# Fused 512-column passes for memory queries, memory keys, u and four query/key pairs, and a plan with longer margins

## The chip, the cores and the metric

The kernel runs on one core of a Trainium2 chip. Its time is the device time of one execution in microseconds (us). Before the change it was 557.04 us, the median of three runs (556.15 to 557.11). One further execution was taken by the hardware profiler; the profile and the trace come from it.

The core's engines run side by side, each with its own queue of instructions, and wait for one another through semaphores. PE (TensorE) does matmuls and writes their results into PSUM, a small memory of 8 banks of 128 partitions x 512 fp32 numbers. DVE (VectorE) and ACT (ScalarE) do the elementwise work and read PSUM and SBUF, POOL (GpSimd) does little here, and SP (SyncE) issues most of the transfers from the chip's main memory.

## The reference

Two layers over x of 256 positions x 1024, each a token mixer beside a cross-attention into 256 memory tokens, an output projection, a LayerNorm, and a SwiGLU feed-forward part with another LayerNorm. Everything is fp32.

```python
for i in range(DEPTH):                       # 2 layers
    if i == 0:
        u, v, q_mem = split(x @ a_w_in, [768, 1536])
        mix = gmlp_mixer(u, v, ...)          # gelu(u) * (W_s layer_norm(gelu(v)) + b), chunks of 128
    else:
        q, k, v, q_mem = split(x @ b_w_in, [768, 1536, 2304])
        mix = moba_attention(q, k, v)        # 12 heads of 64; one block of 256: causal attention
    mem_out = memory_cross_attention(q_mem, mem, w_mem_kv[i])      # 4 heads of 64
    sub = concatenate([mix, mem_out]) @ w_mix_out[i]
    x = layer_norm(ALPHA * x + sub, ...)
    x = layer_norm(ALPHA * x + swiglu(x, w_ffn_in[i], w_ffn_out[i]), ...)   # D_FF 2816
```

## The kernel before

**Precision.** TensorE works on a shorter format (fp32r). So `split(hi, lo, src)` makes two parts of every fp32 operand: ScalarE casts src into hi, VectorE subtracts hi from src into lo. A product is three matmuls into one PSUM tile, `PASSES = ((0, 0), (0, 1), (1, 0))`: hi by hi, hi by lo, lo by hi. In the profile ScalarE's casts and VectorE's subtractions into tiles named `spl_...` are the splits of weights, the costliest groups of both engines.

**Projections.** The projections that come out transposed (features on the partitions, the 256 positions along a row) go through `ws_proj`: for every block of 128 weight columns and each of KT = 8 slices of the model dimension, three matmuls, each with 128x128 weights as the stationary operand and 256 columns of tokens as the moving one:

```python
for j in cols:
    for k in range(KT):
        for n, (a, b) in enumerate(PASSES):
            mm(pst[:, j % pst.shape[1], :], stream.rows(w, k, KT)[:, a, j * P:(j + 1) * P], xs(b, k), ...)
```

The token tile xT (x2T in layer 1) holds hi and lo of a slice next to each other, 512 columns in all; memT, the memory tokens, held them as (hi or lo, slice, position) before. `ws_proj` makes the memory queries (tiles hqm; from them qqm, scaled and split by `stack_q`), the memory keys (hkm; kkm and klm by `stack_k`), u of layer 0 (pu; then gelu into uT) and the queries and keys of layer 1 (qk). Each pair hp of heads in layer 1 takes two blocks of 128 columns, `qk_half(hp, 0)` the queries and `qk_half(hp, 1)` the keys; `stack_q` and `stack_k` make hi (ScalarE, into qks) and lo (VectorE, into qks and klq) of them out of PSUM, and `scores` multiplies them (tiles s).

**Stages, with their place in the profiled span.** v of layer 0 until 22.45 us, then hqm, u, hkm, the gMLP gate (sv), values of the memory (pvm) and scores (sm); from 61.88 the output projection of layer 0 (opa), one `step` for each slice of 128 mixed features and one half (tt) of the positions, with its last slices in `close`, and between the steps the memory attention's transposes (ptm) and its products with the values (pvm); LayerNorm; from about 100 the feed-forward part of layer 0. There `product` forms seven Strassen-like products for each pair of column chunks (M1 to M7, tiles Xf, Yf, Zf), `m1f` and `m5f` are the gated results (m5f by a VectorE instruction that wants sgf from ScalarE), `tpf` their transposes on TensorE, htf the split transposes, and fof the output sums. Layer 1 begins at about 262 (bv, then hqm at 291.74, qk and attention until 345) and ends with its own output projection (opc) and feed-forward part (names in g).

**The order.** Nothing runs as the code is written, except on TensorE. `Plan` records every instruction, and `Plan.order` then simulates the kernel with a cost for each instruction and a model of the transfers (`Wire`). TensorE's order is the program's. For the other engines `simulate` takes, whenever an engine is free, the ready instruction with the earliest due time, or lets a more urgent one that is soon ready go first, depending on three numbers (slip, idle, margin). It does so for every entry of `TRIALS` and keeps the order in which TensorE loses least by the model. `Wire.SPARE` is the margin, in ns, by which a transfer from SyncE or from GpSimd is taken to land later than modelled. Copies and scalings (`nc.copy`, `nc.scale`) may go to ScalarE or to VectorE, and the plan chooses. All planned instructions are issued on one line, L590, so the profile's rows must be told apart by their tiles.

Of the kernel before, what the change touches and what calls it, by code (L numbers as in the profile page):

```python
# [13 lines left out]
F32 = mybir.dt.float32  # L14
F32R = mybir.dt.float32r
BF16 = mybir.dt.bfloat16
AF = mybir.ActivationFunctionType
# [4 lines left out]
P = 128  # L22
D = 1024
T = 256
# [222 lines left out]
class Wire:  # L247

    HARD, SOFT, BOTH, LANES = ((7000, 250), (30000, 370), (1e12, 428)), 223, (155, 123), 8
    SPARE, SKEW = (600, 800), 2000  # L250

    def __init__(self):
        self.now, self.hard, self.soft, self.sent = 0.0, [], [], []
# [36 lines left out]
class Plan:  # L290


    ENGINES = ("tensor", "vector", "scalar", "gpsimd", "sync")
    TRIALS = ((150, 1500, 800), (150, 1000, 500), (300, 1500, 1200), (100, 700, 300), (300, 2500, 1600))

    def __init__(self, nc, pools, space):
        self.nc, self.pools, self.space, self.ops, self.trials = nc, pools, space, [], []
# [102 lines left out]
    def simulate(self, slip, idle, margin):  # L400
# [73 lines left out]
        while len(out) < len(self.ops):  # L474
            best, again = None, False
            for e in self.ENGINES:
                if e == "tensor":
                    if ip == len(pe) or waiting[pe[ip].n]:
                        continue
                    cands = [pe[ip]]  # L480
                else:
                    cands = ready[e]
                c = [(max(free[e], t), op) for op in cands for t in (opening(op, e),) if t is not None]
                if not c:
                    continue
                t0 = min(t for t, _ in c)
                first = [x for x in c if x[0] <= t0 + 1]
                t, op = min(first, key=lambda x: (x[1].late, x[1].n))

                me = op.calls()[e]  # L490
                if e in by_late:
                    u = by_late[e]
                    while head[e] < len(u) and u[head[e]] in gone:
                        head[e] += 1
                    soon, memo = None, {}
                    for o2 in u[head[e]:head[e] + 40]:
                        if o2.late >= op.late:
                            break
                        if o2 in gone or not waiting[o2.n] or t + me.hold <= o2.late + lost - margin:
                            continue  # L500
                        r = hope(o2, memo, 4)
                        if t < r < t + me.hold and (soon is None or r < soon[0]):
                            soon = r, o2
                    for t2, o2 in c:
                        if t < t2 < t + me.hold and o2.late < op.late and t + me.hold > o2.late + lost - margin and (
                                soon is None or t2 < soon[0]):
                            soon = t2, o2
                    if soon:
                        r, o2 = soon
                        short = [x for x in c if x[0] + x[1].calls()[e].hold <= r + slip and x[1] is not op]  # L510
                        if short:
                            t, op = min(short, key=lambda x: (x[1].late, x[1].n))
                        elif r + o2.hold + me.hold < op.late + lost and r - busy[e] < idle:
# [170 lines left out]
def build(chip, tc, ins, out):  # L684
    ET = mybir.EngineType
    with (
# [18 lines left out]
        def mm_tile(name):  # L705
            return tile_of("ps", [P, 512], F32, "mm", name, 4)
# [78 lines left out]
        def ws_proj(pst, w, xs, cols=(0, 1)):  # L785
# [4 lines that stand above are left out]
                        mm(pst[:, j % pst.shape[1], :], stream.rows(w, k, KT)[:, a, j * P:(j + 1) * P], xs(b, k),  # L790
                           k == 0 and n == 0, k == KT - 1 and n == 2)

        def ts_pass(pst, xs, wsl, tt, first, last):

            for n, (a, b) in enumerate(PASSES):
                mm(pst, xs(a)[:, tt * P:(tt + 1) * P], wsl(b), first and n == 0, last and n == 2)
# [155 lines left out]
            stream.done(name)  # L952
            return t

        def mem_q(name, xs):
            qa = [tile_of("act", [P, 2, T], F32R, f"qm{c}", f"q{name}{c}") for c in range(2)]
            t = proj_t(name, xs)
            for c in range(2):
                stack_q(lambda par: qa[c][:, par, :], t[:, c, :])
            return qa  # L960

        def mem_k(name, memx):
            ka = [tile_of("act", [P, 2, T], F32R, f"mix{6 + c}", f"k{name}{c}") for c in range(2)]
            t = proj_t(name, memx)
            for c in range(2):
                stack_k(lambda par: ka[c][:, par, :], klm[:, c], t[:, c, :])
            return ka, klm

        def acc_mms(acc, lhs, rhs, first, last):
# [263 lines left out]
        memT = []  # L1233

        def memx(s, k):
            return memT[k // 2][:, s, k % 2, :]

        stream.get("qm0", 1)
        gv = raw_tile("gv").rearrange("p (a c) -> p a c", a=2)[:, :, :W_MIX]
# [23 lines left out]
        qm = mem_q("qm0", xs)  # L1263
        stv = [sm(f"stv{tt}", 18)[:, :12] for tt in range(2)]
        for h in range(2):
            for tt in range(2):
# [2 lines left out]
                nc.vector.bn_stats(stv[tt][:, 6 * h:6 * h + 6], vn[:, tt, sl])  # L1269
        uT = []  # L1270
        for i in range(3):
            pu = mm_tile(f"pu{i}").rearrange("p (j t) -> p j t", j=2)
            ws_proj(pu, f"u{i}", xs)
            stream.done(f"u{i}")
            uT.append(work_tile(f"uT{i}"))
            nc.scalar.activation(uT[i], flat(pu), AF.Gelu_apprx_tanh)
        for j in range(4):
            if j % 2 == 0:
                both = tile_of("spl", [P, 2, 1024], F32R, "spl", f"memT{j}", HALF_BUFS)
            t = both[:, j % 2, :].rearrange("p (s n) -> p s n", s=2)  # L1280
            split(t[:, 0, :], t[:, 1, :], mraws[j])
            memT.append(t.rearrange("p s (k t) -> p s k t", k=2))
        km = mem_k("km0", memx)
        for tt in range(2):
            mv = sm(f"mvv{tt}", 2)
# [33 lines left out]
            nc.sync.dma_start(xres[tt], ins["x"][tt * P:(tt + 1) * P, :])  # L1319
        gb = load_gb(0, "mix")  # L1320
        op.step(0, [2, 3, 4, 5])
        pts = mem_transposes(pr, "0")
        op.step(1, [0], first=True)
        mem_pv(pts, vm, mix, "0")
        op.step(1, [1])
        op.close(0, [6, 7], xres, gb)
        x1T = tile_of("act", [P, KT, 2, T], F32R, "xT", "x1T")
        op.step(1, range(2, 6))
        op.close(1, [6, 7], xres, gb)
        A = {}  # L1330
        transpose_x(0, xres, x1T, "a", A)
# [16 lines left out]
        for tt in range(2):  # L1348
# [189 lines left out]
```

## Time and profile before

| | before |
|---|---|
| time, median of three runs | 557.04 us (556.15 to 557.11) |
| the profiled execution: its time | 556.42 us |
| its span (first to last recorded work) | 554.7 us |
| instructions on DVE / ACT | 665 / 571 |
| DMA, bytes moved | 132.51 MB, mean 239 GB/s |

The rows of the profile name an engine, an operation and tiles (output<-inputs, buffer numbers left out), then shapes and counts. A chain row gives start, length, engine, tile and number; a timeline row start, length, engine, line, operation, tiles, number, and in brackets idle time ahead of it with what ended it.

### The profile page before, as it was taken

Reading aid. Unit: us, or ns where it says so; the run is one execution under the profiler, and the core shown is the slowest. Engines: PE = TensorE matmul, PEld = TensorE weight load, DVE = VectorE, ACT = ScalarE, POOL = GpSimd, SP = SyncE. Lnnn points to the kernel's source line nnn. Section 1 sums busy time; section 2 is a strip of 40 time slices with the busy share of each in tenths; the row PEclk is TensorE's granted clock in tenths of the full one; section 3 lists DMA queues with packets and bytes.
Section 4 is the critical chain, followed back from the end, with each engine's and each line's share of the span. In section 5 each row is a group of like instructions: output and inputs, shape, how many; then the busy total and the mean of one; then the engine's idle time right before and its main releaser. Section 6 shows DMA issues by size and latency. Waiting matters only on the chain.

```text
span 554.7 us, 7993 instructions
## 1 busy us (share of the span) xinstructions
PE 545.8 (98%) x3028; PEld 473.4 (85%) x3028; DVE 502.1 (91%) x665; ACT 371.0 (67%) x571; POOL 34.3 (6%) x45
## 2 busy tenths in 40 slices
PE   9999999999999999999999999999999999999994
PEld 8999979888888888787899999888788888888884
DVE  5899969999999998989996888889999999989985
ACT  6867846785748495766555999846857585857620
POOL 2120000000000010000000000100000000001001
PEclk9999999999999999999999999999999999999998
DMA  8999843666897969889658232692678989797902
GB/s 294 403 384 381 330 171 115 191 186 222 200 421 165 380 178 324 273 251 353 231 206 325 77 114 78 211 283 77 161 259 223 419 158 417 160 371 201 284 1 77
DMA packets 23494, 132.51 MB, mean 239 GB/s; under 512 B 2592, under 2 KB 6304, under 8 KB 9376
## 3 DMA queue, kind: packets, MB, share of 16 engines
q1 hardware_dynamic: 20000, 109.45, 50.5%
q0 software_dynamic: 3024, 22.02, 21.3%
q8 instruction: 24, 0.39, 0.3%
q10 hardware_dynamic: 432, 0.52, 0.3%
q14 instruction: 14, 0.11, 0.1%
HBM read 120.46 MB, written 1.05 MB: 219 GB/s over the span
## 4 chain that ended last, share of the span: by engine, by line
PE 72%; DVE 14%; DMA 7%; issue 4%; ACT 2%; SPq 0%; DVEq 0%; ACTq 0%; POOLq 0%
PE fog L590 11%; PE Xg L590 10%; DVE spl_s_M L590 7%; PE qk L590 6%; PE Zg L590 5%; DMA raw_s<-in_w 4%; PE opc L590 4%; PE opa L590 4%; PE pu L590 3%; PE bv L590 3%; PE pvm L590 3%; PE Yg L590 2%; PE va L590 2%; PE hkm L590 2%; PE hqm L590 2%
## 5 line engine op out<-in xcount | busy, mean ns | idle before, releaser
L590 DVE TENSOR_TENSOR spl_s_M<-raw_s,spl_s_M 128x1024 fp32r<-128x1024 f32 x140 | 164.7, 1221 | 6.3 <-ACT spl_s_M L590 6.1
L590 ACT CAST spl_s_M<-raw_s 128x1024 fp32r<-128x1024 f32 x140 | 139.6, 1050 | 38.1 <-DMA raw_s<-in_w 23.4
L590 PE MATMUL fof<-spl_w,htf 128*128 128x512 f32 x264 | 63.9, 392 | 0.0
L590 PE MATMUL fog<-spl_w,htg 128*128 128x512 f32 (+1 forms) x282 | 63.9, 378 | 0.0
L590 ACT CAST spl_w<-raw_w 128x1024 fp32r<-128x1024 f32 x44 | 45.6, 1051 | 23.4 <-DMA raw_w<-in_w 20.9
L590 PEld LDWEIGHTS fog<-spl_w,htg 128*128 128x128 f32 x282 | 50.2, 188 | 9.4
L590 PEld LDWEIGHTS fof<-spl_w,htf 128*128 128x128 f32 x264 | 49.0, 188 | 9.9
L590 DVE TENSOR_TENSOR spl_w<-raw_w,spl_w 128x1024 fp32r<-128x1024 f32 x44 | 53.7, 1221 | 2.9 <-ACT spl_w L590 2.9
L590 DVE TENSOR_TENSOR raw_s<-raw_s,raw_s 128x2048 f32<-128x2048 f32 x19 | 43.5, 2288 | 0.1
L590 PE MATMUL qk<-x2T,spl_qk 128*128 128x256 f32 x288 | 36.3, 283 | 0.0
L590 PEld LDWEIGHTS qk<-x2T,spl_qk 128*128 128x128 f32 x288 | 35.2, 192 | 0.0
L590 PE MATMUL Zg<-spl_s_M,SgM 128*128 128x512 f32 x120 | 29.1, 390 | 0.0
L590 PE MATMUL Xg<-spl_s_M,SgM 128*128 128x512 f32 x120 | 29.0, 390 | 0.0
L590 PE MATMUL Zf<-spl_s_M,SfM 128*128 128x512 f32 x120 | 29.0, 390 | 0.0
L590 PE MATMUL Xf<-spl_s_M,SfM 128*128 128x512 f32 x120 | 28.8, 389 | 0.0
L590 PE MATMUL Xf<-spl_s_M,x1T 128*128 128x512 f32 x120 | 28.3, 390 | 0.0
L590 PE MATMUL Xg<-spl_s_M,x3T 128*128 128x512 f32 x120 | 28.3, 390 | 0.1
L590 PEld LDWEIGHTS Xf<-spl_s_M,x1T 128*128 128x128 f32 x120 | 22.4, 188 | 5.2 <-issue 0.6
L590 PEld LDWEIGHTS Xg<-spl_s_M,x3T 128*128 128x128 f32 x120 | 22.5, 188 | 5.1 <-issue 0.4
L590 PEld LDWEIGHTS Zg<-spl_s_M,SgM 128*128 128x128 f32 x120 | 22.5, 188 | 5.0 <-DVE SgM L590 0.4
L590 PEld LDWEIGHTS Xf<-spl_s_M,SfM 128*128 128x128 f32 x120 | 22.5, 188 | 4.7
L590 PEld LDWEIGHTS Xg<-spl_s_M,SgM 128*128 128x128 f32 x120 | 22.4, 188 | 4.8 <-DVE SgM L590 0.2
(246 smaller groups left out, 1007.8 us busy)
## 6 DMA issues: line engine op xcount, KB each, us to landing
raw_s<-in_w SPq DMA_DIRECT2D x40, 1024.0 KB, 7.7
raw_w<-in_w SPq DMA_DIRECT2D x22, 1024.0 KB, 8.6
raw_s<-in_w POOLq DMA_DIRECT2D x11, 1024.0 KB, 9.0
raw_s<-raw_s POOLq DMA_DIRECT2D x10, 1024.0 KB, 7.6
raw_o<-in_w SPq DMA_DIRECT2D x8, 1024.0 KB, 7.7
raw_qk<-in_w SPq DMA_DIRECT2D x6, 1024.0 KB, 5.4
raw_u<-in_w SPq DMA_DIRECT2D x3, 1024.0 KB, 11.6
raw_bv<-in_w SPq DMA_DIRECT2D x4, 768.0 KB, 8.1
```

Source lines behind the costliest of these rows:

```text
L590: getattr(getattr(self.nc, c.engine), c.name)(*map(real, c.args), **{k: real(v) for k, v in c.kw.items()})
```

## The change

`joint` takes the place of `ws_proj` in 22 blocks of 128 weight columns: for each slice, one matmul of weight hi by the 512 columns token hi and token lo, then one of weight lo by the 256 columns token hi, into the first half of the PSUM tile. A copy (on ScalarE or VectorE) takes the second half out and a VectorE add adds the first to it, in an SBUF tile `sum_...` (three buffers; for u the tile uT itself). `stack_q`, `stack_k` and the gelu then read SBUF. The last two pairs of heads (hp 4 and 5) stay as they were. memT is laid out anew, so that hi and lo of a slice are 512 columns in a row. `SPARE`, `TRIALS` and a rule of `simulate` change too, and in layer 0 the memory transposes and the products with the values come in two pieces.

```diff
-    SPARE, SKEW = (600, 800), 2000
+    SPARE, SKEW = (1600, 2000), 2000
...
-    TRIALS = ((150, 1500, 800), (150, 1000, 500), (300, 1500, 1200), (100, 700, 300), (300, 2500, 1600))
+    TRIALS = ((0, 700, 100), (150, 700, 100), (150, 700, 300), (0, 700, 500), (150, 700, 500))
...
-                me = op.calls()[e]
+                hold = op.calls()[e].hold
+                if e == "scalar" and op.name == "activation" and op.args[2] not in (AF.Identity, table):
+                    hold += 1283
...
+        def joint(name, w, xk, j, tile, out):
+
+            pst = tile(name)
+            for k in range(KT):
+                rw = stream.rows(w, k, KT)[:, :, j * P:(j + 1) * P]
+                mm(pst, rw[:, 0], xk(k).rearrange("p s t -> p (s t)"), k == 0, False)
+                mm(pst[:, :T], rw[:, 1], xk(k)[:, 0, :], False, k == KT - 1)
+            nc.copy(out, pst[:, T:])
+            nc.vector.tensor_add(out, out, pst[:, :T])
+
+        def sum_tile(name):
+            return tile_of("act", [P, T], F32, "sum", f"sum_{name}", 3)
...
-            t = proj_t(name, xs)
             for c in range(2):
-                stack_q(lambda par: qa[c][:, par, :], t[:, c, :])
+                t = sum_tile(f"{name}{c}")
+                joint(f"h{name}{c}", name, xk, c, mm_tile, t)
+                stack_q(lambda par: qa[c][:, par, :], t)
...
-            pu = mm_tile(f"pu{i}").rearrange("p (j t) -> p j t", j=2)
-            ws_proj(pu, f"u{i}", xs)
+            uT.append(work_tile(f"uT{i}"))
+            for j in range(2):
+                half = uT[i][:, j * T:(j + 1) * T]
+                joint(f"pu{i}{j}", f"u{i}", lambda k: xT[:, k], j, mm_tile, half)
+                nc.scalar.activation(half, half, AF.Gelu_apprx_tanh)
             stream.done(f"u{i}")
-            uT.append(work_tile(f"uT{i}"))
-            nc.scalar.activation(uT[i], flat(pu), AF.Gelu_apprx_tanh)
...
-            t = both[:, j % 2, :].rearrange("p (s n) -> p s n", s=2)
-            split(t[:, 0, :], t[:, 1, :], mraws[j])
-            memT.append(t.rearrange("p s (k t) -> p s k t", k=2))
+            t = both[:, j % 2, :].rearrange("p (k s t) -> p k s t", k=2, s=2)
+            split(t[:, :, 0, :], t[:, :, 1, :], mraws[j].rearrange("p (k t) -> p k t", k=2))
+            memT.append(t)
...
-        pts = mem_transposes(pr, "0")
+        pts = mem_transposes(pr, "0", (0, 1))
         op.step(1, [0], first=True)
-        mem_pv(pts, vm, mix, "0")
+        pts += mem_transposes(pr, "0", (2, 3))
+        mem_pv(pts, vm, mix, "0", (0,))
         op.step(1, [1])
+        mem_pv(pts, vm, mix, "0", (1,))
+        op.step(1, [2])
         op.close(0, [6, 7], xres, gb)
...
-        qm = mem_q("qm1", xs)
+        qm = mem_q("qm1", lambda k: x2T[:, k])
...
-            t = (acc_tile if j else mm_tile)(f"qk{hp}{j}")[:, :T].rearrange("p (j t) -> p j t", j=1)
-            ws_proj(t, f"qk{hp}", xs, (j,))
-            t = t[:, 0, :]
+            if hp < 4:
+                t = sum_tile(f"qk{hp}{j}")
+                joint(f"qk{hp}{j}", f"qk{hp}", lambda k: x2T[:, k], j, acc_tile if j else mm_tile, t)
+            else:
+                t = (acc_tile if j else mm_tile)(f"qk{hp}{j}")[:, :T].rearrange("p (j t) -> p j t", j=1)
+                ws_proj(t, f"qk{hp}", xs, (j,))
+                t = t[:, 0, :]
```

(`mem_k` changes like `mem_q`.)

Three places show what the change does to the order of the engines. The first is TensorE in layer 0's output projection, after step 5 of the first half of the positions. opa are the two PSUM tiles of the second half, pm the softmax of one memory head, pTm its transpose in SBUF, svm the memory's values; equal rows that follow in the same group of three passes are left out. Before:

```order
L590 MATMUL ptm_927<-ident,pm_843 128x128 x4
L590 MATMUL ptm_932<-ident,pm_867 128x128 x4
L590 MATMUL ptm_939<-ident,pm_879 128x128 x4
L590 MATMUL ptm_946<-ident,pm_895 128x128 x4
L590 MATMUL opa_953<-spl_o_0_0_595,mix_0_764 128x512
L590 MATMUL opa_957<-spl_o_0_0_595,mix_0_764 128x512
L590 MATMUL pvm_963<-pTm_935,svm_864 64x256
L590 MATMUL pvm_963<-pTm_942,svm_864 64x256
L590 MATMUL pvm_970<-pTm_949,svm_864 64x256
L590 MATMUL pvm_970<-pTm_955,svm_864 64x256
L590 MATMUL opa_953<-spl_o_0_1_605,mix_1_769 128x512
L590 MATMUL opa_957<-spl_o_0_1_605,mix_1_769 128x512
```

Of the changed kernel:

```order
L592 MATMUL ptm_861<-ident,pm_821 128x128 x4
L592 MATMUL ptm_871<-ident,pm_840 128x128 x4
L592 MATMUL opa_878<-spl_o_0_0_565,mix_0_697 128x512
L592 MATMUL opa_882<-spl_o_0_0_565,mix_0_697 128x512
L592 MATMUL ptm_894<-ident,pm_851 128x128 x4
L592 MATMUL ptm_901<-ident,pm_864 128x128 x4
L592 MATMUL pvm_906<-pTm_880,svm_784 64x256
L592 MATMUL pvm_906<-pTm_884,svm_784 64x256
L592 MATMUL opa_878<-spl_o_0_1_580,mix_1_704 128x512
L592 MATMUL opa_882<-spl_o_0_1_580,mix_1_704 128x512
L592 MATMUL pvm_928<-pTm_908,svm_784 64x256
L592 MATMUL pvm_928<-pTm_911,svm_784 64x256
```

The four heads' transposes are two and two now, with a step of the output projection between them, and the two products pvm are a step apart.

The second place is VectorE in the feed-forward part of layer 0, where chunk 7's m5f is gated (the row SCALAR_TENSOR_TENSOR). spl_w_7_0 is a weight of the output sums, raw_s and spl_s_9_M are weights of the next pair's products. Before:

```order
L590 TENSOR_TENSOR spl_w_7_0_2172<-raw_w_7_2101,spl_w_7_0_2172 128x1024
L590 TENSOR_TENSOR raw_s_9_11_2091<-raw_s_9_11_2091,raw_s_9_12_2117 128x2048
L590 TENSOR_TENSOR spl_s_9_M_0_2201<-raw_s_9_21_2138,spl_s_9_M_0_2201 128x1024
L590 SCALAR_TENSOR_TENSOR m5f_2056<-m5f_2056,sgf_2211 128x512
L590 TENSOR_TENSOR spl_s_9_M_0_2217<-raw_s_9_11_2091,spl_s_9_M_0_2217 128x1024
L590 TENSOR_TENSOR spl_s_9_M_1_2224<-raw_s_9_11_2091,spl_s_9_M_1_2224 128x1024
```

Of the changed kernel:

```order
L592 TENSOR_TENSOR spl_w_7_0_2123<-raw_w_7_2046,spl_w_7_0_2123 128x1024
L592 TENSOR_TENSOR raw_s_9_11_2038<-raw_s_9_11_2038,raw_s_9_12_2062 128x2048
L592 SCALAR_TENSOR_TENSOR m5f_2003<-m5f_2003,sgf_2151 128x512
L592 TENSOR_TENSOR spl_s_9_M_0_2156<-raw_s_9_21_2082,spl_s_9_M_0_2156 128x1024
L592 TENSOR_TENSOR spl_s_9_M_0_2164<-raw_s_9_11_2038,spl_s_9_M_0_2164 128x1024
L592 TENSOR_TENSOR spl_s_9_M_1_2171<-raw_s_9_11_2038,spl_s_9_M_1_2171 128x1024
```

m5f has moved up by one weight split.

The third is the same instruction for the last pair of that part, chunk 9, among the splits of the weights of v in layer 1 (spl_bv). Before:

```order
L590 TENSOR_TENSOR spl_w_10_1_2408<-raw_w_10_2328,spl_w_10_1_2408 128x1024
L590 TENSOR_TENSOR spl_bv_0_2417<-raw_bv_2344,spl_bv_0_2417 128x768
L590 TENSOR_TENSOR spl_bv_1_2425<-raw_bv_2344,spl_bv_1_2425 128x768
L590 TENSOR_TENSOR spl_bv_0_2457<-raw_bv_2380,spl_bv_0_2457 128x768
L590 SCALAR_TENSOR_TENSOR m5f_2311<-m5f_2311,sgf_2469 128x512
L590 TENSOR_TENSOR spl_bv_1_2474<-raw_bv_2380,spl_bv_1_2474 128x768
```

Of the changed kernel:

```order
L592 TENSOR_TENSOR spl_w_10_1_2361<-raw_w_10_2276,spl_w_10_1_2361 128x1024
L592 TENSOR_TENSOR spl_bv_0_2381<-raw_bv_2292,spl_bv_0_2381 128x768
L592 TENSOR_TENSOR spl_bv_1_2387<-raw_bv_2292,spl_bv_1_2387 128x768
L592 SCALAR_TENSOR_TENSOR m5f_2251<-m5f_2251,sgf_2407 128x512
L592 TENSOR_TENSOR spl_bv_0_2412<-raw_bv_2323,spl_bv_0_2412 128x768
L592 TENSOR_TENSOR spl_bv_1_2420<-raw_bv_2323,spl_bv_1_2420 128x768
```

Here, too, one weight split stands behind m5f now that stood ahead of it.

Elsewhere, VectorE has 22 adds and 11 copies more (of sum_qm three, sum_km two, sum_qk six), and 8 copies of 512 columns in the feed-forward parts and of svm went from VectorE to ScalarE. ScalarE also has the other 11 copies (six of uT, one sum_qm, two sum_km, two sum_qk). On SyncE's queue layer 0's raw_vm stands behind two loads of bs, and xres ahead of gb0mix.

More of the change, by code (lines that the diff above doesn't have):

```diff
@@ L498, in simulate @@
                             break
-                        if o2 in gone or not waiting[o2.n] or t + me.hold <= o2.late + lost - margin:
+                        if o2 in gone or not waiting[o2.n] or t + hold <= o2.late + lost - margin:
                             continue
                         r = hope(o2, memo, 4)
-                        if t < r < t + me.hold and (soon is None or r < soon[0]):
+                        if t < r < t + hold and (soon is None or r < soon[0]):
                             soon = r, o2
                     for t2, o2 in c:
-                        if t < t2 < t + me.hold and o2.late < op.late and t + me.hold > o2.late + lost - margin and (
+                        if t < t2 < t + hold and o2.late < op.late and t + hold > o2.late + lost - margin and (
                                 soon is None or t2 < soon[0]):
@@ L512, in simulate @@
                             t, op = min(short, key=lambda x: (x[1].late, x[1].n))
-                        elif r + o2.hold + me.hold < op.late + lost and r - busy[e] < idle:
+                        elif r + o2.hold + hold < op.late + lost and r - busy[e] < idle + hold - op.calls()[e].hold:
                             free[e] = r
@@ L953, in proj_t, with mem_q @@
             return t
-        def mem_q(name, xs):
+        def mem_q(name, xk):
             qa = [tile_of("act", [P, 2, T], F32R, f"qm{c}", f"q{name}{c}") for c in range(2)]
-            t = proj_t(name, xs)
             for c in range(2):
-                stack_q(lambda par: qa[c][:, par, :], t[:, c, :])
+                t = sum_tile(f"{name}{c}")
+                joint(f"h{name}{c}", name, xk, c, mm_tile, t)
+                stack_q(lambda par: qa[c][:, par, :], t)
+            stream.done(name)
             return qa
@@ L963, in mem_k @@
             ka = [tile_of("act", [P, 2, T], F32R, f"mix{6 + c}", f"k{name}{c}") for c in range(2)]
-            t = proj_t(name, memx)
             for c in range(2):
-                stack_k(lambda par: ka[c][:, par, :], klm[:, c], t[:, c, :])
+                t = sum_tile(f"{name}{c}")
+                joint(f"h{name}{c}", name, lambda k: memT[k // 2][:, k % 2], c, mm_tile, t)
+                stack_k(lambda par: ka[c][:, par, :], klm[:, c], t)
+            stream.done(name)
             return ka, klm
@@ L1235, in memx @@
         def memx(s, k):
-            return memT[k // 2][:, s, k % 2, :]
+            return memT[k // 2][:, k % 2, s, :]
         stream.get("qm0", 1)
@@ L1261, in build @@
                 nc.sync.dma_start(bsB[i][j * HD:(j + 1) * HD], ins["bs"][j:j + 1, 2 * i:2 * i + 2, :].to_broadcast([HD, 2, P]))
-        qm = mem_q("qm0", xs)
+        qm = mem_q("qm0", lambda k: xT[:, k])
         stv = [sm(f"stv{tt}", 18)[:, :12] for tt in range(2)]
@@ L1321, in build @@
         op.step(0, [2, 3, 4, 5])
-        pts = mem_transposes(pr, "0")
+        pts = mem_transposes(pr, "0", (0, 1))
         op.step(1, [0], first=True)
-        mem_pv(pts, vm, mix, "0")
+        pts += mem_transposes(pr, "0", (2, 3))
+        mem_pv(pts, vm, mix, "0", (0,))
         op.step(1, [1])
+        mem_pv(pts, vm, mix, "0", (1,))
+        op.step(1, [2])
         op.close(0, [6, 7], xres, gb)
         x1T = tile_of("act", [P, KT, 2, T], F32R, "xT", "x1T")
-        op.step(1, range(2, 6))
+        op.step(1, range(3, 6))
         op.close(1, [6, 7], xres, gb)
```

## The prediction

> **What bounds the kernel now.** I read the page's busy times first.
>
> ```profile
> span 554.7 us, 7993 instructions
> ## 1 busy us (share of the span) xinstructions
> PE 545.8 (98%) x3028; PEld 473.4 (85%) x3028; DVE 502.1 (91%) x665; ACT 371.0 (67%) x571; POOL 34.3 (6%) x45
> ```
>
> TensorE (PE) is busy 98% of the span, VectorE (DVE) 91%, ScalarE (ACT) 67%. A busy share says nothing of who waits for whom, so next comes the view of waits for TensorE: what it waited for, the total, how often, the longest.
>
> ```profile
> PE warmup L744 <- DVE mhalf L741: 1.1, 1, 1.1
> PE tpf L590 <- DVE m5f L590: 0.7, 2, 0.4
> ```
>
> After its start TensorE waits in two places only, both for one product tile of the feed-forward part of layer 0. So the time is the sum of TensorE's instructions, plus a start and an end that the change hardly touches. A change can win by giving TensorE less to do or by removing those two waits, and it loses when VectorE or ScalarE no longer deliver in time. VectorE has 554.7 - 502.1 = 52.6 us of idle time in all, unevenly spread.
>
> What does one matmul cost? Consecutive matmuls overlap, so their own durations mislead; the chain of work that ended last gives steps (start, length, line, number of matmuls):
>
> ```profile
> 22.45 5.75 PE hqm L590 x48
> 28.20 17.28 PE pu L590 x144
> ...
> 282.36 9.37 PE bv L590 x54
> ...
> 374.74 2.72 PE Xg L590 x12
> ```
>
> The matmuls of hqm and pu have 256 columns: 5.75 / 48 = 119.8 ns. Those of bv have 384: 9.37 / 54 = 173.5 ns. Those of Xg have 512: 2.72 / 12 = 226.7 ns. The three lie on a line: 0.4176 ns a column, and 226.7 - 512 x 0.4176 = 12.9, so **about 13 ns for each matmul whatever its width**.
>
> **The change, part by part.**
>
> *Fused matmuls.* A projection block of 128 weight columns had, for each of 8 slices of the model dimension, three matmuls of 256 columns. Now it has one of 512 and one of 256. The columns are the same, the matmuls 16 instead of 24. A block cost 24 x 119.8 = 2875 ns and costs 8 x (226.7 + 119.8) = 2772 ns: 0.103 us less. There are 22 blocks (2 + 2 + 2 + 2 for the memory queries and keys of both layers, 6 for u, 8 for four pairs of queries and keys): -2.3 us (176 matmuls by 13 ns). All of it is on the path, since TensorE sets the end. I take **-2.3**.
>
> *What the fused form adds beside it.* The two halves of the result must be added: a 256-column copy out of PSUM (22, on ScalarE or VectorE; 11 went to each) and a VectorE add (22). For the add the nearest row is VectorE's sum of a PSUM tile and an SBUF tile; for a 512-column copy, the second row (both by line and form, 22 to 95 us):
>
> ```profile
> L590 DVE TENSOR_TENSOR mix<-pvm,mix 128x256 fp32r<-128x256 f32 x2 | 0.8, 418 | 0.0
> L590 DVE COPY svm<-pvm 128x512 f32<-128x512 f32 x1 | 0.7, 689 | 0.0
> ```
>
> VectorE's instructions overlap a little: in its timeline, below, one starts at 227.78 and lasts 1.22 us, and the next starts at 228.91, 0.09 before that end. So a further 256-column one costs 0.42 - 0.09 = 0.33 us. No row shows a 256-column copy on VectorE; it lies below the 0.69 of 512 columns, and I take it like the add. VectorE gets 22 + 11 = 33 of these, 33 x 0.33 = +11 us. The new plan also moves 8 copies of 512 columns from VectorE to ScalarE, 8 x (0.69 - 0.09) = -4.8 us (their new places are on ScalarE, 67% busy), so VectorE is about 6 us busier, against 52.6 idle. Whether it hides is read by stage (from:to, length, then busy time and number on PE, PEld, DVE, ACT, POOL; clock; DMA):
>
> ```profile
> 22.45:28.20 5.75, 5.75 (x51) 5.75 (x50) 5.33 (x9) 5.42 (x8) 1.49 (x1) 1.00 1.06 396
> 28.20:61.88 33.68, 33.68 (x306) 33.38 (x305) 32.97 (x45) 24.26 (x39) 2.81 (x2) 1.00 1.02 389
> 61.88:87.56 25.68, 25.68 (x131) 20.67 (x130) 20.95 (x38) 16.24 (x33) 0.99 (x1) 1.00 0.46 167
> 291.74:309.93 18.19, 18.19 (x154) 18.19 (x154) 12.40 (x28) 11.35 (x25) 0.00 (x0) 1.00 0.61 236
> 309.93:345.47 35.54, 35.54 (x306) 34.67 (x307) 30.42 (x92) 34.94 (x99) 0.00 (x0) 1.00 0.30 104
> ```
>
> Layer 0, 22.45 to 87.56: VectorE is busy 5.33 + 32.97 + 20.95 = 59.25 of 65.11 us, idle 5.9; there fall 10 adds and 3 copies, 4.3 us. It fits, narrowly, and 4.7 of the idle 5.9 are behind 61.88, so what is ready early today (the split weights spl_o of the output projection) becomes ready later. Layer 1, 291.74 to 345.47: idle 5.79 + 5.12 = 10.9; there fall 10 adds and 8 copies, 5.9 us. ScalarE, 34.94 of 35.54 in the last stage, is the fuller one there, and it gets only two of the eight query and key copies. In layer 0 it has the room (24.26 of 33.68 us) for six copies of u and for u's activations, now six of 256 columns for three of 512. So the direct cost is nothing as long as the idle time lies where it is needed; with that cover gone it is the whole 6 us (the second rival).
>
> *The first scores of layer 1* are the tightest chain: the block of keys, its copy and add, then ScalarE's casts and VectorE's low parts klq, then the scores. The three rows are of VectorE's and ScalarE's timelines and of the chain:
>
> ```profile
> 304.83 0.87 DVE L590 TENSOR_TENSOR klq<-qk,qks 64x256 fp32r<-64x256 f32 x2 [1.28 <-ACT qks L590]
> ```
>
> ```profile
> 303.28 1.52 ACT L590 CAST qks<-qk 64x256 fp32r<-64x256 f32 x4 [0.99 <-PE qk L590]
> ```
>
> ```profile
> 306.12 0.93 PE s L590 x8
> ```
>
> Today klq starts at 304.83, behind all four casts (303.28 + 1.52 = 304.80), and ends at 305.70, 0.42 before the scores. Both engines read one PSUM tile, and the trace shows them one after the other. From the SBUF sum they need not be: the first klq wants the first cast only, the second the third cast. The chain gets 0.42 + 0.42 longer by copy and add, and shorter by two or three casts (some 0.38 each, 0.8 to 1.1) that now run beside klq. I take 0; the margin of 0.42 covers a loss of that size, and the bounds are -0.4 (nothing left to win, since TensorE does not wait here) and +0.5 (0.84 added, no overlap won, 0.42 covered).
>
> *The two waits for m5f.* The timelines of TensorE, VectorE and ScalarE:
>
> ```profile
> 229.09 0.27 PE L590 MATMUL tpf<-ident,m1f 128*128 128x128 f32 x1
> 229.65 0.33 PE L590 MATMUL tpf<-ident,m5f 128*128 128x128 f32 x1 [0.30 <-DVE m5f L590]
> 229.82 0.27 PE L590 MATMUL tpf<-ident,m1f 128*128 128x128 f32 x1
> ...
> 261.73 0.66 PE L590 MATMUL tpf<-ident,m5f 128*128 128x128 f32 x4 [0.36 <-DVE m5f L590]
> ```
>
> ```profile
> 227.78 1.22 DVE L590 TENSOR_TENSOR spl_s_M<-raw_s,spl_s_M 128x1024 fp32r<-128x1024 f32 x1
> 228.91 0.69 DVE L590 SCALAR_TENSOR_TENSOR m5f<-m5f,sgf 128x512 f32<-128x512 f32 x1
> ...
> 258.38 2.69 DVE L590 TENSOR_TENSOR spl_bv<-raw_bv,spl_bv 128x768 fp32r<-128x768 f32 x3
> 260.98 0.69 DVE L590 SCALAR_TENSOR_TENSOR m5f<-m5f,sgf 128x512 f32<-128x512 f32 x1
> ```
>
> ```profile
> 226.62 0.59 ACT L590 ACTIVATE sgf<-Xf 128x512 f32<-128x512 f32 x1
> ...
> 258.85 0.59 ACT L590 ACTIVATE sgf<-Xf 128x512 f32<-128x512 f32 x1
> ```
>
> The transpose at 229.65 comes 0.56 us behind the one at 229.09, where its successors come 0.11 apart: 0.45 lost. At 261.73 I count 0.5 likewise (the gap of 0.36, and the refilling of the pipeline that the first place shows on top). VectorE had the operand sgf at 227.2 and 259.4 but ran a weight split first. The new order puts m5f ahead of that split both times (rows of VectorE above): 228.91 - 227.78 = 1.13 us earlier, and 2.69 / 3 = 0.9 us earlier, against 0.45 and 0.5. What is late next is the split itself, one m5f (0.6 us) later, and its weights are wanted only after the transposes. So **-0.95**; bounds 0 and -0.95.
>
> *Memory attention of layer 0 in pairs.* The transposes and the products with the values come in two pieces each, between steps of the output projection.
>
> ```profile
> 70.07 1.75 PE ptm L590 x16
> 71.82 1.40 PE opa L590 x6
> 73.22 1.88 PE pvm L590 x16
> 75.09 12.47 PE opa L590 x54
> ```
>
> After ptm six opa take 1.40 where 6 x 226.7 = 1.36: 0.04 for the change of form. After pvm 54 take 12.47 where 12.24 are due: 0.23. One more exit of each kind is +0.27, and I add 0.08 for one more entry, an estimate of the size of the small exit: **+0.35** (bounds 0.2 and 0.5). In return each pvm stands behind at least two more steps after its transposes; today nobody waits here, so this wins nothing directly.
>
> *The plan itself.* Wider margins for transfers, another list of trials and a surcharge for changing ScalarE's function table shift hundreds of VectorE and ScalarE instructions by a few places, and a few DMA issues on SyncE's and GpSimd's queues (layer 0's raw_vm behind two small bias loads, xres ahead of a row of layer-norm factors), none of which was what TensorE waited for. The trace of before cannot price that. Below lies 0 (no wait is left to win but the two counted). Above, the nearest row is the wait for m5f: such waits cost 0.45 to 0.5 us each. I take one of them, **+0.5**, and for the upper end four, +2; likeliest where VectorE is full already:
>
> ```profile
> 87.56:100.81 13.25, 13.25 (x114) 13.25 (x112) 13.18 (x22) 9.60 (x20) 0.99 (x1) 1.00 0.60 231
> 374.70:403.60 28.90, 28.90 (x134) 23.60 (x133) 28.64 (x38) 20.50 (x27) 1.87 (x2) 1.00 0.44 135
> ```
>
> **The sum.** The profiled execution took 556.42 us (a span of 554.7 and 1.7 around it): 556.42 - 2.3 - 0.95 + 0.35 + 0.5 = 554.0. The median of the three other runs is 557.04, 0.62 higher, and by it the sum gives 554.6. I take **554.3**, between them.
>
> **The rivals.**
>
> *More new waits than won.* VectorE's 4.3 us in layer 0 fall for the most part where it has 0.7 us free (28.20 to 61.88), its output is late by the sum of its delays, and TensorE waits 2 to 3.5 us somewhere behind 61.88. For it: those rows. Against it: the idle 4.7 us that follow, where work done early today could as well be done later. Time 555.8 to 557.3, near 556.5. Chance 0.17, most of it within 0.2% of before.
>
> *VectorE becomes the bound: slower.* If the added 6 us of VectorE all delay TensorE, because the idle time sits behind the adds in each stage and cannot be used ahead, the time is 556.42 - 2.3 - 0.95 + 0.35 + 6 = 559.5. It decides from about 3 us of delays that are not absorbed (equal to before), and shows as slower from 4.1. Place: VectorE at spl_o before 61.88, and the sums and klq of 297 to 345. For it: 91% busy. Against it: 10.9 us idle in layer 1. Chance 0.08.
>
> *The fused pair saves nothing.* If a 512-column matmul next to a 256-column one costs as its columns alone, 0.468 ns each as 119.8 / 256 gives, a block takes 8 x 768 x 0.468 = 2875 ns as before, and the time is 556.42 - 0.95 + 0.35 + 0.5 = 556.3. Against it: the rows of bv and Xg, which show the 13 ns. But no row shows the two widths alternating. Chance 0.05.
>
> The Trainium skill speaks for this rival: "TensorE: Matmul & The Clock Gate", section "Wait — 56ns, not 53.3ns?", gives a fixed cost of only about 2.5 ns for a warm back-to-back matmul. By it, as an estimate, 176 fewer matmuls would save 0.44 us and the time would be near 555.9. The rows here, 13 ns at three widths with a granted clock of 1.00, disagree with it.
>
> **How the numbers follow.** Forecast 0.70 (553 to 555.8), rivals 0.17, 0.08 and 0.05. The lower end is the sum with no new wait, 553.5, less 0.7 for the spread of the runs (556.15 to 557.11): 552.8. The upper end takes in most of the first rival: 557.0. A measurement of this kernel tells about 0.2% or 1.1 us from no change, so faster means below 555.9: 0.70 less a few hundredths, and the lower part of the rivals, 0.74. Same (555.9 to 558.2) 0.18, slower 0.08.
>
> **What would show it.** In the chain, 16 matmuls of hqm take 2.77 us a block, pu 16.6 instead of 17.28. TensorE's waits for m5f are gone, its busy time falls by about 2 us. VectorE's busy time rises to about 508, ScalarE's by some 7. If the forecast is wrong, the waits view of TensorE has new rows of over 1 us, on spl_o, mix or klq; if the fused pair saves nothing, pu still takes 17.3.

## The result, and the profile after

The changed kernel takes **554.11 us** (median of five runs, 553.58 to 555.00) where the kernel before took 557.04 (five runs, 556.15 to 558.28). The ratio is 0.9946 with a 95% interval of 0.993 to 0.9962, so it is faster, by 0.54% (2.9 us). The profiled execution took 554.15 us. The forecast was 554.3, within 552.8 to 557.0. One of the nine runs of the kernel named "twice" below took 1111.15 us, where the others took 555.76 to 556.33, and the ratio given for it is that of the other eight.

The page of the changed kernel, the same part as before:

```profile
span 552.1 us, 7664 instructions
## 1 busy us (share of the span) xinstructions
PE 543.3 (98%) x2852; PEld 464.2 (84%) x2852; DVE 509.3 (92%) x692; ACT 378.5 (69%) x591; POOL 33.5 (6%) x45
```

TensorE has 176 matmuls less and is 2.5 us less busy, VectorE is 7 us busier, ScalarE 7.5. TensorE's waits (what waited for what: total us, times, longest):

```profile
PE warmup L746 <- DVE mhalf L743: 1.1, 1, 1.1
PE va L592 <- ACT spl_v L592: 0.4, 1, 0.4
PE va L592 <- ACT x0T L592: 0.3, 1, 0.3
```

The two waits for m5f are gone and no new one has come, except in the first stage, va, which the change does not touch. That stage has to be set apart before anything can be read. va ends, and hqm begins, at 23.60 us, against 22.45 before; in the fourteen profiles of this study that point lies anywhere from 22.45 to 24.42. The first twenty or so instructions of SyncE, ScalarE and VectorE stand in the same order in all of these kernels; what differs is when the first transfers land (the chain's row for raw_v, from 3.12 on, takes 3.86 us before, where hqm begins at 22.45, and 5.83 in all_joint, where it begins at 24.42). So I use **the stretch from the first hqm matmul to the end of TensorE's last matmul**, which leaves the start out. Each end of it is a row of the chain of work. Of the kernel before, its last row:

```profile
536.53 11.18 PE fog L590 x66
```

536.53 + 11.18 - 22.45 = 525.26 us. Of the changed kernel (start, length, tile, number of matmuls):

```profile
23.60 5.55 PE hqm L592 x32
29.15 16.64 PE pu L592 x96
45.79 5.55 PE hkm L592 x32
...
70.16 0.87 PE ptm L592 x8
71.04 1.40 PE opa L592 x6
72.43 0.87 PE ptm L592 x8
73.31 1.01 PE pvm L592 x8
74.32 1.59 PE opa L592 x6
75.91 1.01 PE pvm L592 x8
76.92 11.13 PE opa L592 x48
...
296.15 8.32 PE qk L592 x48
304.47 0.93 PE s L592 x8
305.39 2.83 PE qk L592 x16
...
533.92 11.20 PE fog L592 x66
```

533.92 + 11.20 - 23.60 = 521.52 us. The stretch became **3.74 us** shorter, more than the 2.9 between the medians. In the profiled pair 1.15 us of it was lost at the start again, and some 0.3 around the span (554.15 - 552.1 against 556.42 - 554.7); what the 0.3 is, no run shows.

A block of 16 matmuls takes 5.55 / 2 = 2.775 us, as the sum had it (2.772). pu takes 16.64 instead of 17.28. The steps between ptm and the end of opa (70.16 to 88.05) are 0.4 us longer for the split.

How the stretch divides, by the chain's rows at the stages' borders: 1.06 less from hqm to the output projection (ten blocks), 0.40 more up to the LayerNorm's transposes (the split), 0.21 less at the memory keys of layer 1 (the second row hkm, two blocks), 1.43 less in the feed-forward part of layer 0, 0.81 less in layer 1's queries, keys and attention (ten blocks), 0.64 less in its feed-forward part; the rest within 0.01.

The 1.43 + 0.64 in the feed-forward parts, where the change does nothing but order, are waits that are gone. Two are those for m5f. TensorE's timeline of the changed kernel at the first place:

```profile
229.31 0.27 PE L592 MATMUL tpf<-ident,m1f 128*128 128x128 f32 x1
229.42 0.27 PE L592 MATMUL tpf<-ident,m5f 128*128 128x128 f32 x1
```

and VectorE's:

```profile
227.56 0.69 DVE L592 SCALAR_TENSOR_TENSOR m5f<-m5f,sgf 128x512 f32<-128x512 f32 x1
228.35 2.36 DVE L592 TENSOR_TENSOR spl_s_M<-raw_s,spl_s_M 128x1024 fp32r<-128x1024 f32 x2
```

The m5f transpose now follows 0.11 us behind its neighbour (0.56 before), for m5f ends at 228.25, over 1 us before its transpose, and the weight splits stand behind it. The others are shorter, and TensorE's view of waits does not list them. They show only when a group of like matmuls takes longer than its fellows. The chain of the kernel before:

```profile
395.14 2.81 PE Xg L590 x12
397.95 2.96 PE Zg L590 x12
...
499.06 5.70 PE Xg L590 x24
```

The same groups in the chain of the changed kernel:

```profile
393.19 2.77 PE Xg L592 x12
395.97 2.72 PE Zg L592 x12
...
496.75 5.44 PE Xg L592 x24
```

Twelve matmuls of 512 columns take 2.72; Zg at 397.95 took 0.24 more, Xg at 499.06 0.26 more than its 5.44, and an Xf group at 255.68 began some 0.2 late. None of these delays is left.

Section 4 of the page, the shares of the chain that ended last, says the same in another way. Before:

```profile
PE 72%; DVE 14%; DMA 7%; issue 4%; ACT 2%; SPq 0%; DVEq 0%; ACTq 0%; POOLq 0%
```

and of the changed kernel:

```profile
PE 97%; DMA 1%; DVE 1%; SPq 0%; issue 0%; ACT 0%; DVEq 0%
```

Before, the chain left TensorE at the wait at 261.73 and ran back over VectorE's work and over transfers as far as 123.74 us. Now it stays on TensorE from va to the last matmul.

### The profile page after: what moved, and what is told of

Same layout as the page of the kernel before. It is cut to its first block, busy times and chain, and to the rows that moved or that the text cites. A ratio compares the mean times of both kernels' runs of the same rounds, so it can differ in the third digit from the quotient of the medians.

```text
span 552.1 us, 7664 instructions
## 1 busy us (share of the span) xinstructions
PE 543.3 (98%) x2852; PEld 464.2 (84%) x2852; DVE 509.3 (92%) x692; ACT 378.5 (69%) x591; POOL 33.5 (6%) x45
## 4 chain that ended last, share of the span: by engine, by line
PE 97%; DMA 1%; DVE 1%; SPq 0%; issue 0%; ACT 0%; DVEq 0%
PE fog L592 11%; PE fof L592 11%; PE Xg L592 10%; PE Xf L592 10%; PE qk L592 6%; PE Zf L592 5%; PE Zg L592 5%; PE opa L592 4%; PE opc L592 4%; PE bv L592 3%; PE pu L592 3%; PE pvm L592 3%; PE Yg L592 2%; PE Yf L592 2%; PE va L592 2%; PE hkm L592 2%
## 5 line engine op out<-in xcount | busy, mean ns | idle before, releaser
L592 PE MATMUL qk<-x2T,spl_qk 128*128 128x512 f32 (+1 forms) x224 | 35.7, 315 | 0.0
L592 PEld LDWEIGHTS qk<-x2T,spl_qk 128*128 128x128 f32 x224 | 31.3, 190 | 2.6
```

The costliest lines, as they stand in the source:

```text
L592: getattr(getattr(self.nc, c.engine), c.name)(*map(real, c.args), **{k: real(v) for k, v in c.kw.items()})
```

## The experiments

All stretches are from the first hqm matmul to TensorE's last, in us. Medians, with the ratio to the kernel before timed beside it, are given where a kernel ran more than once; the others ran once, under the profiler.

| kernel | stretch | hqm begins | median (ratio, 95%) |
|---|---|---|---|
| before | 525.26 | 22.45 | 557.04 |
| before_again | 525.10 | 23.66 | |
| changed | 521.52 | 23.60 | 554.11 (0.9946, 0.993 to 0.9962) |
| after_again | 521.53 | 22.59 | |
| joint_only | 523.93 | 23.10 | 555.82 (0.9978, 0.9967 to 0.9988) |
| plan_only | 523.20 | 23.24 | 555.27 (0.9963, 0.995 to 0.9976) |
| no_pairs | 521.96 | 23.10 | 553.81 (0.9942, 0.9929 to 0.9956) |
| all_joint | 522.21 | 24.42 | 554.39 (0.9955, 0.994 to 0.997) |
| old_plan | 523.42 | 23.51 | 555.63 (0.9963, 0.9948 to 0.9978) |
| twice | 523.78 | 23.15 | 556.08 (0.9978, 0.9967 to 0.9988) |
| copies_dve | 522.94 | 23.11 | |
| copies_act | 522.14 | 23.16 | |
| spare_only | 523.19 | 24.05 | |
| trials_only | 523.52 | 23.04 | |

**Is a stretch of one profile worth anything?** Both kernels were profiled again.

> The kernel before, unchanged, profiled a second time. If its small waits belong to its order, they come again at the same five places (about 229, 255, 261, 395 to 398, 499), with the stretch from hqm to TensorE's end within 0.3 us of 525.26, while the start ahead of hqm (22.45) may differ by up to 2 us with the landing of the first transfers. If they are chance, they stand elsewhere and the stretch differs by 0.5 us or more.

> The changed kernel, unchanged, profiled a second time: by the order's account the stretch is within 0.3 us of 521.52 and TensorE waits for nobody behind the start; by chance's account a wait of 0.3 us or more appears.

The stretches came out as 525.10 and 521.53, within 0.16 and 0.01 of the first ones, while the start moved by 1.2 and 1.0 us. The waits of before came at the same places (the one at 499 with 0.1 in place of 0.2). So they belong to the order, and differences in the stretch of some 0.2 us can be read from single profiles, which differences in the total time cannot.

**The fused blocks alone.** The changed kernel with `SPARE`, `TRIALS`, the rule for `hold` and the order of layer 0 put back:

```diff
-    SPARE, SKEW = (1600, 2000), 2000
+    SPARE, SKEW = (600, 800), 2000
...
-                if e == "scalar" and op.name == "activation" and op.args[2] not in (AF.Identity, table):
-                    hold += 1283
...
-        pts = mem_transposes(pr, "0", (0, 1))
+        pts = mem_transposes(pr, "0")
...
```

> The fused blocks alone, with the old margins, trials and rule of the plan and the old order of layer 0's memory attention. Measure: the stretch from the first hqm matmul to the end of TensorE's last matmul, 525.26 us before (22.45 to 547.71), 521.52 after (23.60 to 545.12). Theory A (TensorE's steps bound the kernel, the fused blocks save their 13 ns a matmul, the small waits belong to the plan): TensorE's steps get 2.1 us shorter as in the changed kernel, and waits of 0.5 to 2 us remain or appear in the feed-forward parts; stretch 522.5 to 524, time 1 to 2.5 us below before. Rival B (the fused blocks give nothing; the plan gave it all): stretch 525 or more, time as before. Rival C (without wider margins VectorE's extra adds make TensorE wait): new rows of over 1 us in TensorE's waits, stretch above 525.

523.93: 1.33 less than before. TensorE's steps are shorter as in the changed kernel, by about 2.1, but it waits some 0.8 more in the feed-forward part of layer 1 than the kernel before did. Its waits behind the start:

```profile
PE tpg L590 <- DVE m1g L590: 0.7, 1, 0.7
PE Xf L590 <- DVE m5f L590: 0.4, 1, 0.4
PE tpf L590 <- DVE m5f L590: 0.3, 1, 0.3
PE tpg L590 <- DVE m5g L590: 0.3, 1, 0.3
```

Theory A holds. The stage with the adds, up to 90 us, shows no wait, so rival C is out; but with this plan the blocks bring 1.33 and not the 2.1 by which the steps got shorter.

**The plan alone.** The kernel before with `SPARE`, `TRIALS` and the rule of the changed one:

```diff
-    SPARE, SKEW = (600, 800), 2000
+    SPARE, SKEW = (1600, 2000), 2000
...
-    TRIALS = ((150, 1500, 800), (150, 1000, 500), (300, 1500, 1200), (100, 700, 300), (300, 2500, 1600))
+    TRIALS = ((0, 700, 100), (150, 700, 100), (150, 700, 300), (0, 700, 500), (150, 700, 500))
...
+                if e == "scalar" and op.name == "activation" and op.args[2] not in (AF.Identity, table):
+                    hold += 1283
...
```

> The new margins, trials and rule of the plan alone, with the old three passes of 256 columns and the old order of layer 0. Theory A: TensorE's steps stay as before, its small waits of before (0.45 at 229, 0.29 at 255, 0.52 at 261, 0.29 at 395 to 398, 0.30 at 499, in all about 1.85 us) go for the most part; stretch 523.4 to 524.2, time 1 to 1.9 us below before. Rival B (the plan gave it all): stretch 521.5 to 522, time 3 us below before. Rival D (the waits go only because the fused blocks shift the work): the waits stay or stand elsewhere, stretch 525 or more.

523.20, 2.06 less, a little beyond theory A's 1.85 and just outside its range, and TensorE's waits are gone; what is left of the view is the start:

```profile
PE warmup L746 <- DVE mhalf L743: 1.1, 1, 1.1
PE va L592 <- ACT spl_v L592: 0.6, 1, 0.6
```

The ratios of the two halves, 0.9978 and 0.9963, give 0.9941 as a product. Both together without the split (no_pairs, below) have 0.9942, and the whole change has 0.9946.

**The fused blocks with the old plan** (only `SPARE`, `TRIALS` and the rule put back; the split of layer 0 stays):

> The changed kernel with the old margins, trials and rule of the plan (fused blocks and split memory attention stay). Theory A (the waits in the feed-forward parts are a matter of the plan): TensorE waits 1 to 2 us in all for m5f, m1g or m5g, as it did with the old plan twice (before 1.9 us, the fused blocks alone 2.4 us), stretch 522.5 to 523.9. Rival D (the old plan's waits came by chance of one order, and the split frees enough): no such row, stretch 521.5 to 521.8.

523.42. Again TensorE waits for m1g, m5g and m5f (0.7, 0.3 and 0.2 in its view). With the fused blocks and the split the new plan is worth 523.42 - 521.52 = 1.90, without them 2.06. The stretch is 0.51 shorter than joint_only's, although the stage with the split is 0.40 longer: the waits in the feed-forward part of layer 0, two in joint_only's view, are fewer. An edit in one stage shifts the waits of another.

**Which edit of the plan?** The kernel before with one of the two edits of numbers each:

> The kernel before with the wider margins for transfers alone (old trials, old rule). If the margins are what took the five waits away (a weight that is taken to land later is split later, so that m5f goes ahead of it), the stretch is 523.0 to 523.6; if the trials or the surcharge for ScalarE's table did it, waits stay and the stretch is 524.5 or more.

> The kernel before with the new list of trials alone (old margins, old rule). If shorter waits for an urgent instruction took the waits away, the stretch is 523.0 to 523.6; if the margins did it, waits stay and the stretch is 524.5 or more.

523.19 and 523.52: each alone does all or most of it (2.07 and 1.74 of 2.06), which neither expectation had allowed for. trials_only still waits at one place, in its timeline of TensorE:

```profile
410.52 0.27 PE L590 MATMUL tpg<-ident,m1g 128*128 128x128 f32 x1
411.03 0.33 PE L590 MATMUL tpg<-ident,m5g 128*128 128x128 f32 x1 [0.24 <-DVE m5g L590]
```

What the surcharge for ScalarE's table is worth by itself wasn't tried.

**Without the split in layer 0.**

```diff
-        pts = mem_transposes(pr, "0", (0, 1))
+        pts = mem_transposes(pr, "0")
         op.step(1, [0], first=True)
-        pts += mem_transposes(pr, "0", (2, 3))
-        mem_pv(pts, vm, mix, "0", (0,))
+        mem_pv(pts, vm, mix, "0")
         op.step(1, [1])
-        mem_pv(pts, vm, mix, "0", (1,))
-        op.step(1, [2])
...
```

> The changed kernel with layer 0's memory transposes and products in one piece each, as before. Theory A: the split costs its two extra changes of form and wins nothing, so the stretch gets 0.35 to 0.4 shorter, 521.1, and TensorE still waits for nobody; time 0.4 below the changed kernel. Rival E (the split is what keeps TensorE from waiting for pTm or mix there, since VectorE is later now): a row of TensorE's waits at opa or pvm between 70 and 90 us of 0.4 or more, stretch 521.6 or more.

521.96: 0.44 longer, not 0.4 shorter. Rival E has the number and the stage, but the wait stands at ptm, for pm, and not at opa or pvm, for pTm or mix, and the view of waits lists only 0.2 of it. Its timeline of TensorE:

```profile
69.49 1.47 PE L592 MATMUL ptm<-ident,pm 128*128 128x128 f32 x12
71.17 0.84 PE L592 MATMUL ptm<-ident,pm 128*128 128x128 f32 x4 [0.21 <-ACT pm L592]
```

The fourth head's transposes wait for its softmax pm: they begin at 71.17, 0.21 us after the twelve before them have ended, where they usually overlap. From the first opa to the LayerNorm's transposes it takes 26.28 us, where the kernel before took 25.68 without a wait and the changed one 26.08 with the split. So the split's price of 0.4 is right, and it buys off a loss of 0.6 there, 0.2 net. The other 0.24 stands in the feed-forward part of layer 0, where a group that takes 5.44 in the changed kernel takes 5.67 in the chain:

```profile
162.06 5.67 PE Xf L592 x24
```

But joint_only, with the same unsplit order and the old plan, takes 25.68 from opa to the LayerNorm's transposes: the wait is made by how the new plan with the adds orders that stage, not by the adds as such. By time (0.9942 against 0.9946) the two can't be told apart.

**All six pairs fused.**

```diff
-            if hp < 4:
+            if hp < 6:
                 t = sum_tile(f"qk{hp}{j}")
```

> The changed kernel with the last two pairs of heads (hp 4 and 5) fused as well: 4 blocks more. Theory A: 4 x (2.88 - 2.83) to 4 x 0.10 = 0.2 to 0.4 us less, stretch 521.1 to 521.3, TensorE waits nowhere. Rival C (VectorE and ScalarE are full between 310 and 345): TensorE waits 0.3 to 2 us at s or pt of the last pairs, stretch 521.5 to 523.5.

522.21, 0.69 longer. The attention stage is 0.24 shorter as theory A had it, and the view shows no wait of TensorE there; the number lies in rival C's range, but not for rival C's reason. Some 0.1 is lost at a pt among the opc steps, and 0.8 in the feed-forward part of layer 1. TensorE's timeline there:

```profile
410.49 0.33 PE L592 MATMUL tpg<-ident,m1g 128*128 128x128 f32 x1 [0.22 <-DVE m1g L592]
411.09 0.33 PE L592 MATMUL tpg<-ident,m5g 128*128 128x128 f32 x1 [0.27 <-DVE m5g L592]
```

In the 17 us before m1g VectorE's order is the same as in the changed kernel, but it comes to m1g 0.8 us later relative to TensorE. It has more to do ahead of that: one weight split (spl_r_B) that the changed kernel has done before the feed-forward part begins, and a copy of 0.67 us,

```profile
376.30 0.67 DVE L592 COPY m1g<-Xg 128x512 f32<-128x512 f32 x1
```

which the changed kernel gives to ScalarE:

```profile
375.54 0.59 ACT L592 COPY m1g<-Xg 128x512 f32<-128x512 f32 x1 [1.00 <-PE Xg L592]
```

By the window view VectorE is busy 27.67 of the 28.61 us from 372.79 on in the changed kernel, so whoever is late there stays late. joint_only, old_plan and trials_only lose time at this place too. It is one of two tight places; the other is the Xf group at 162 in layer 0, late in joint_only, old_plan, no_pairs and copies_act.

**How much room has VectorE?** One more VectorE instruction in each fused block, and then all copies on VectorE or all on ScalarE:

```diff
+            nc.vector.tensor_scalar_mul(out, out, 1.0)
```

> The changed kernel with one more VectorE instruction in each of the 22 fused blocks, a product of the sum with 1.0 in place, 0.35 us each, 7.7 us in all; it also lengthens every chain from a block to its scores or gate by 0.35. VectorE would be busy some 517 us of 552. Theory A (VectorE's idle time still hides the adds, with room): stretch 521.5 to 522.5. Rival C (VectorE is close to the bound: it decides from about 3 us of work that is not absorbed): TensorE waits 2 to 7 us, stretch 523.5 to 529, at layer 0's opa or layer 1's s.

```diff
-            nc.copy(out, pst[:, T:])
+            nc.vector.tensor_copy(out, pst[:, T:])
```

> The changed kernel with all 22 copies of the second half on VectorE (11 of them were on ScalarE): VectorE +11 x 0.33 = 3.6 us. Theory A: no difference beyond what the plan's order shifts, stretch 521.5 to 522.3. Rival C: TensorE waits 1 to 4 us, in layer 0 between 45 and 90 us first, where VectorE has least room, stretch 522.5 to 525.

```diff
-            nc.copy(out, pst[:, T:])
+            nc.scalar.copy(out, pst[:, T:])
```

> The changed kernel with all 22 copies on ScalarE (11 of them were on VectorE): VectorE -3.6 us, ScalarE +3 us, of which 1.7 us between 290 and 345, where ScalarE was busy 47.5 of 54.2 us. Theory A: stretch 521.4 to 522. Rival F (ScalarE holds up the scores of layer 1): TensorE waits 0.3 to 2 us at s or pt, stretch 522 to 523.5.

twice: 523.78, so of 7.7 us more work 2.3 came through. That is outside theory A's range and inside rival C's: VectorE is close to the bound. Its waits behind the start:

```profile
PE ptm L592 <- ACT pm L592: 0.5, 1, 0.5
PE s L592 <- ACT qks L592: 0.3, 1, 0.3
```

copies_dve: 522.94, so of 3.6 us 1.4 came through, again by rival C: 1.1 of them before the LayerNorm's transposes, at ptm, and 0.2 in the feed-forward part of layer 0. The wait at ptm:

```profile
PE ptm L592 <- DVE pm L592: 0.6, 1, 0.6
```

copies_act: 522.14, 0.6 longer, though VectorE has less to do; the scores of layer 1 don't wait (rival F is out), and the delays stand in the feed-forward part of layer 0 (0.17 at a tpf, 0.28 at an Xf), where the order has shifted once more. The number lies in rival F's range, but neither expectation had this place. I read it as the scatter that any shift of the plan brings; that is not shown.

## Why the prediction was right

*TensorE's steps bound the kernel.* Right in the changed kernel: where blocks were fused, the stages got shorter by what TensorE was given less of, to a few hundredths (1.06 for ten blocks of 0.103). With the old plan a part of it goes into new waits (joint_only, 1.33 of 2.1).

*The fused blocks: 2.3.* The mechanism is right, 13 ns a matmul also where 512 and 256 columns alternate, which no row of before showed: 5.55 / 32 = 173.4 ns, the mean of 226.7 and 119.8 being 173.3. The rival that a fused pair saves nothing is out. The Trainium skill ("TensorE: Matmul & The Clock Gate", section "Wait — 56ns, not 53.3ns?") gives about 2.5 ns, by which, as an estimate, the blocks would have saved 0.44; the steps measured in this kernel's stream disagree with it. The measured sum is 2.07, not 2.3. The sum took every block at 0.103, but four of the five key and query groups that follow scores (s, sm) or transposes save 0.05: 16 matmuls take 2.83 at 305.39, where a block in a run of blocks takes 2.77.

*The adds and copies: nothing.* Right for the changed kernel, with less to spare in layer 0 than the sum left, and only beside the new plan and the split: without the split TensorE loses 0.6 at ptm, and with the old plan 0.8 more in the feed-forward part of layer 1. Whether the adds themselves or the order that comes with them makes these losses, no run separates. The windows of the changed kernel (VectorE is the third busy time):

```profile
23.60:29.15 5.55, 5.55 (x34) 4.89 (x33) 4.46 (x10) 5.55 (x9) 2.02 (x2) 1.00 1.05 399
29.15:61.97 32.82, 32.82 (x242) 29.82 (x241) 32.37 (x48) 26.41 (x47) 1.60 (x1) 1.00 0.89 320
61.97:88.05 26.08, 26.08 (x131) 20.55 (x130) 24.63 (x44) 16.36 (x33) 0.98 (x1) 1.00 0.67 256
```

In these rows it is idle 64.45 - 61.46 = 3.0 us, where it was 5.9 before. Behind 61.97 it is idle 1.45 in place of 4.7: work moved back into the idle time there, as supposed. Twice and copies_dve show how near the edge is: of what is added from here on, three to four tenths come through (2.3 of 7.7 and 1.4 of 3.6), though some of that may be the order's scatter, since copies_act lost 0.6 with less work for VectorE. The rival of VectorE as the bound, which makes all of it come through, is false here.

*The first scores of layer 1: 0.* Right. VectorE's timeline:

```profile
302.19 0.42 DVE L592 TENSOR_TENSOR sum_qk<-sum_qk,qk 128x256 f32<-128x256 f32 x1
303.08 0.42 DVE L592 TENSOR_TENSOR klq<-sum_qk,qks 64x256 fp32r<-64x256 f32 x1 [0.47 <-ACT qks L592]
303.94 0.42 DVE L592 TENSOR_TENSOR klq<-sum_qk,qks 64x256 fp32r<-64x256 f32 x1 [0.44 <-ACT qks L592]
```

and ScalarE's:

```profile
302.64 1.69 ACT L592 CAST qks<-sum_qk 64x256 fp32r<-64x256 f32 x4 [0.44 <-DVE sum_qk L592]
```

The low parts klq now run between the casts, the first behind the first cast, the second behind the third, where they had to wait for all four. The last ends at 304.36; the second head's scores, which want it, begin near 304.8. So 0.4 is left, as before. A chain 0.35 longer per block (twice) makes the scores wait.

*The two waits for m5f: 0.95.* Right in cause and size; gone in both profiles of the changed kernel and in plan_only.

*The split: +0.35.* It costs 0.40. That it wins nothing was wrong for the kernel as changed: without it the new plan loses 0.6 us waiting for pm.

*The plan: +0.5.* **This is the step that failed.** It rested on "no wait is left to win but the two counted", which was read from the waits view. There were 0.9 to 1.1 us more, in delays of 0.1 to 0.3 us each that the view left out, and the new plan took them too; nor did the new wait come. On the stretch the sum gave -2.4 and the chip -3.74. That the total still met the forecast so closely is luck: the two profiled executions started unevenly, 1.15 us to the disadvantage of the changed kernel. With an even start and the same time around the span, the profiled 556.42 would have become 552.7, just below the range. Between the medians of five it is 2.9, near the forecast's 2.7; the medians of the kernel before with more runs (557.47 of 23, 557.36 of 13), taken beside other kernels than the changed one, would make it some 3.3.

Counted by stage, of the 3.74 about 2.07 are the fused blocks, 2.07 the waits that went with the plan, and 0.40 is the split's price. The parts are not worth the same one by one: without the new plan the kernel loses 1.90, without the split 0.44, and the fused blocks alone bring 1.33. Why either edit of the plan alone takes the waits away stays open.

## What to carry to other kernels

Where the engine that bounds a kernel is busy 98%, count what it is given: a fixed price per instruction read off three widths predicted a mixture that the trace of before did not have, to 0.2 of 2.3 us. Before saying that it waits nowhere, compare equal groups of its instructions, since the delays of 0.1 to 0.3 us stood in no list of waits here. And where the start is set by the first transfers, compare kernels from a point behind it; here the rest repeated to 0.2 us. Where instructions are ordered by a plan, take each part out once with the others in place, since the parts did not add up.

## What the runs showed of the hardware

The first matmuls behind pvm, which has fp32 operands, are late: 48 opa steps take 11.13 us where 48 x 226.7 ns are 10.88, 0.25 more. The block of 2.83 us behind scores is another case. Its operands are fp32r like those of the scores, and the loss is not at its front: in TensorE's timeline its first matmul starts at 305.23, its ninth at 306.64 and the next group at 308.06, so both halves are equally slow, 1.41 and 1.42 where 2.77 / 2 is 1.39. The same blocks are slow in the second profile. Why is open. One program is repeated more exactly than its total time suggests: the stretch agreed to 0.01 us between two profiles of the changed kernel and to 0.16 between two of the kernel before, while the landing of the first transfers moved the start by up to 2.0 us (22.45 to 24.42).
